# Six token groups of a gated unit join the attention phase's event loop, and the first loads of the phase before it move ahead

## The chip, the cores and the metric

The kernel runs on one core of one Trainium2 chip. The metric is the device time of one execution of the whole program, in microseconds (us). The core has five engines with a queue of instructions each, worked off in order: TensorE (PE in the profile; PEld is its weight load), VectorE (DVE), ScalarE (ACT), GpSimd (POOL) and SyncE (SP), which here only issues transfers. Transfers (DMA) run beside them, on 16 engines of their own. A timing of this kernel tells a change of about 0.2% (5 us) from none.

## The reference, cut to what matters

One layer of a decoder trunk on 2048 tokens of width 1024, in float32. One projection feeds three groups of heads; their normed outputs are joined, multiplied by `w_out`, added to `x`, and a squared-ReLU feed-forward follows.

```python
proj = rms_norm(x, norm1_g) @ w_in
o_a = swa_sink_mixer(qa, ka, va, sinks, bias[:, :4])      # banded attention, window 128
# o_b: a state-space scan, then the gated unit:
z = gelu(y);  ab = z @ glu_w + glu_b                       # 512 -> 1024
o_b = ab[..., :512] * sigmoid(ab[..., 512:])
# o_c: compressed blocks, top-16 selected blocks, window 512, gated and summed
o_c = nsa_mixer(qc, kvc, gates, cmp_pos, cmp_w1, cmp_w2, ..., bias[:, 4:])
mixed = concat(rms_norm(o_a), rms_norm(o_b), rms_norm(o_c))
x = x + mixed @ w_out
x = x + relu(rms_norm(x) @ w_up) ** 2 @ w_down
```

## The kernel before, in words

Products on PE take float32 factors split into a high and a low part, so that one product is three matmuls (`mm3`, L70 to L74). The program is a sequence of phases.

**The front** (`phase_front`, L77) computes the projection for token groups 0 to 15 and writes its columns to DRAM as `pa`, `pb`, `pc` (L169), runs the state-space scan, and leaves the activated result `z` in on-chip memory as `u_st` (L556).

**The middle phase** (in `trunk`, L2239 to L2251) merges three lists of steps by their share of the list (`merge`, L64): the banded attention of 16 blocks of 128 tokens (`swa_steps`: `prep` loads the rows `ta` at L916 and L917 and turns them, then `log_step`, `pv_step`, `close`); the gated unit (`glu_steps`, L575: eight loads of weights, L587 to L592, two of the bias, then for each of the 16 token groups `zt`, which copies the rows on POOL (L608), turns them on PE (L611) and splits them (L614, L615), and two calls of `half`, each of 13 matmuls of 128x512 into one PSUM bank (L72 to L74, L626), followed by a tanh (L629), or by the product (L634), the square sum (L635) and the store to `ob` (L636)); and a third list of the bias tables (`bias_steps`, L677: a table `T` of 1 MB and a table `b_sel` of 0.5 MB for each of four heads, L693 and L694, and the copy of `b_cmp` on POOL, L695) and of the compressed keys (`compress_steps`, L700). Here the Tile framework orders the instructions of each engine: by priority, which is the place in the program, shifted where the code says so, and by when its model of times takes them to be ready. The matmuls of `half` are shifted back by 300 places:

```python
        with tc.high_priority(offset=-FILL_GLU):
```

PSUM has eight banks: six of the banded attention, one (`pm`) of the gated unit, and one (`pg`) which the compressed keys share with the first half-product of groups 0 to 10 (`GLU_SHARES`); groups 11 to 15 use `pm` alone.

**The mixing phase** (`phase_mix`, L1084) has its order written by an event loop (`Flow`, L995) at build time. Each piece of work is a routine (a generator) that yields the events and rings of buffers that it needs and then an operation as a triple of engine, expected time and function; the loop always takes the operation that can start first, and among those the one of lowest rank (L1052 to L1060). Its whole order on every engine is fixed (`manual_schedule`). For each block i of 128 tokens there are routines for the loads and turned heads (`front`), the compressed branch (`compressed`; from block 8 on `select` picks the blocks), the window and the selected branch (`attended`), and the output product (`finished`, `filled`: 48 matmuls into `pw`, L1656). The three branches of a block each fill one bank of the ring `po`, which has two, until a copy to `oT` (L1383) frees it. The output weights `wo` take the memory of the gated unit, so they are loaded only after `open_late` (L1120), which gives that memory back and computes the row factors from the square sums of all groups:

```python
            yield E[0]["w1"]
            yield "DVE", 5000, open_late
            fire(opened, flow.engines["DVE"])
```

`E[0]["w1"]` is the end of block 0. In `open_late` two chains of small DVE operations (L40 to L50, then L1141) read the square sums `ss_a` and `ss_b`; the second waits for the last group of the gated unit. Behind `opened` the weights are loaded in 16 pieces and split on ACT and DVE (L1169, L1170).

**The feed-forward** (`phase_up`, `phase_down`) follows.

## Time and profile before

| what | value |
| --- | --- |
| time, median of 3 runs | 2517.14 us (2515.62 to 2517.17) |
| the profiled execution's own time | 2512.47 us |
| its span in the profile | 2510.4 us |
| PE busy over the span | 2408.8 us, 96% |
| DVE, ACT, POOL busy | 71%, 53%, 41% |
| mean granted clock of PE | 0.986 |
| middle phase, about | 400 to 600 us |
| mixing phase, about | 602 to 1240 us |

Times in the profile count from the start of the span. "PEclk" is the clock that was granted to PE in a stretch, as a share of the full clock. A row of the timeline gives the start, the duration, the engine, the line of the kernel, the operation and its tiles as out<-in, and in brackets how long the engine had been idle and what released it. A row of the table of stretches gives the stretch, its length, and the busy time of each engine in it with the count of its instructions, then PEclk, the share of the transfer engines in use, and GB/s.

### The profile page before, as it was taken

The page shows a single profiled execution, that of the slowest core. Times are in us where ns is not written, and L with a number is a line of the kernel's source. Part 1 is how long each engine was busy: PE and PEld are TensorE (multiplying, and loading weights), DVE is VectorE, ACT ScalarE, POOL GpSimd, SP SyncE. Part 2 cuts the span into 40 slices and gives each one's busy share as a digit, 9 for nine tenths or more (in the row PEclk, how much of TensorE's full clock was granted, in tenths as well). Part 3 has the DMA queues.
Part 4 walks back from the last instruction along what each step waited for, and adds up shares of the span by engine and source line. Part 5 has one row for each costly group of instructions (what it writes and reads, how often), then busy time and mean ns, then how long its engine had stood idle before and what let it go on. Part 6 is the DMA issues. An engine that isn't in the chain of part 4 may idle for free.

```text
span 2510.4 us, 37968 instructions
## 1 busy us (share of the span) xinstructions
PE 2408.8 (96%) x12738; PEld 2064.4 (82%) x12738; DVE 1780.0 (71%) x3496; ACT 1322.1 (53%) x2754; POOL 1037.5 (41%) x1027
## 2 busy tenths in 40 slices
PE   8999998999699999999799999999999999999999
PEld 8899997777588888888678888788887888888887
DVE  7853875864687788878465665755557988888886
ACT  6443545754577667666455555544444444434442
POOL 0000222311243344322656775565664435445447
PEclk9999998999799999999999999999999999999999
DMA  7473325421322233211556667755448443444435
GB/s 231 141 261 108 111 91 183 114 60 47 94 72 74 78 117 114 66 60 45 182 165 192 187 198 219 215 166 156 145 128 280 145 124 98 135 135 127 127 99 197
DMA packets 402259, 344.45 MB, mean 137 GB/s; under 512 B 43622, under 2 KB 359020, under 8 KB 400112
## 3 DMA queue, kind: packets, MB, share of 16 engines
q1 hardware_dynamic: 341840, 288.44, 37.9%
q10 hardware_dynamic: 60224, 53.59, 6.8%
q8 instruction: 100, 1.64, 0.3%
q14 instruction: 95, 0.78, 0.1%
HBM read 227.39 MB, written 119.76 MB: 138 GB/s over the span
## 4 chain that ended last, share of the span: by engine, by line
PE 62%; DVE 3%; DMA 3%; issue 3%; POOL 2%; ACT 2%; ACTq 0%; SPq 0%; DVEq 0%; POOLq 0%
PE pdc L2117 7%; PE pdb L2117 7%; PE pda L2117 7%; PE pub L1938 6%; PE pw L1656 6%; PE puc L1938 6%; PE pua L1938 5%; PE pdd L2117 3%; PE pud L1938 3%; PE pos L1357 2%; PE pps L1324 2%; PE pow L1357 1%; PE pqs L1299 1%; PE pqs L1300 1%; PE ppw L1324 1%
## 5 line engine op out<-in xcount | busy, mean ns | idle before, releaser
L1784 ACT CAST v<-vr 128x512 fp32r<-128x512 f32 x224 | 139.4, 624 | 303.8 <-DMA vr<-vd 126.6
L1785 DVE TENSOR_TENSOR v<-vr,v 128x512 fp32r<-128x512 f32 x224 | 235.1, 1058 | 78.6 <-ACT v L1784 78.3
L2117 PE MATMUL pdc<-dw,v 128*128 128x512 f32 x768 | 187.2, 393 | 4.4 <-ACT dw L1784 2.8
L2117 PE MATMUL pdb<-dw,v 128*128 128x512 f32 x768 | 184.5, 389 | 0.0
L2117 PE MATMUL pda<-dw,v 128*128 128x512 f32 x768 | 184.5, 389 | 0.0
L2117 PEld LDWEIGHTS pdc<-dw,v 128*128 128x128 f32 x768 | 145.4, 190 | 36.1 <-ACT dw L1784 3.3
L546 POOL TENSOR_TENSOR t<-Q,E 128x508 f32<-128x508 f32 x16 | 22.1, 1384 | 364.5 <-PE pbt L517 251.7
L2117 PEld LDWEIGHTS pdb<-dw,v 128*128 128x128 f32 x768 | 144.1, 188 | 30.0
L2117 PEld LDWEIGHTS pda<-dw,v 128*128 128x128 f32 x768 | 144.1, 188 | 29.9
L1784 ACT CAST uh<-fs 128x512 fp32r<-128x512 f32 x124 | 76.3, 621 | 156.3 <-PE pub L1938 59.7
L1785 DVE TENSOR_TENSOR ul<-fs,uh 128x512 fp32r<-128x512 f32 x124 | 130.9, 1057 | 32.5 <-ACT uh L1784 31.9
L1909 POOL TENSOR_TENSOR fs<-ur,ur 128x512 f32<-128x512 f32 x62 | 89.1, 1437 | 156.0 <-DMA ur<-in_w_up 120.7
L1785 DVE TENSOR_TENSOR ul<-ur,uh 128x512 fp32r<-128x512 f32 x93 | 99.4, 1071 | 48.2 <-ACT uh L1784 45.5
L1656 PE MATMUL pw<-wo_h,mh 128*128 128x512 f32 x256 | 105.6, 413 | 11.1 <-ACT pw L1679 10.9
L1340 ACT CAST ths<-pps 128x512 fp32r<-128x512 f32 (+1 forms) x144 | 79.1, 563 | 64.2 <-PE pps L1324 52.9
L1954 POOL TENSOR_TENSOR ev<-e,e 128x512 f32<-128x512 f32 x64 | 90.8, 1419 | 46.1 <-ACT e L1951 19.7
L1345 DVE TENSOR_TENSOR tls<-pps,ths 128x512 fp32r<-128x512 f32 (+1 forms) x144 | 92.8, 656 | 17.2 <-ACT ths L1340 16.2
L1938 PE MATMUL pub<-fh,uh 128*128 128x512 f32 x256 | 101.3, 396 | 3.3 <-DVE e L1947 3.3
L1656 PE MATMUL pw<-wo_l,mh 128*128 128x512 f32 x256 | 104.0, 406 | 0.0
L1656 PE MATMUL pw<-wo_h,ml 128*128 128x512 f32 x256 | 103.9, 406 | 0.0
L1938 PE MATMUL puc<-fh,uh 128*128 128x512 f32 x256 | 100.3, 392 | 2.1 <-DVE eu L1947 1.9
L1938 PE MATMUL pua<-fh,uh 128*128 128x512 f32 x256 | 99.7, 389 | 1.5 <-ACT pw L1679 1.5
(556 smaller groups left out, 7788.5 us busy)
## 6 DMA issues: line engine op xcount, KB each, us to landing
vr<-vd SPq DMA_DIRECT2D x224, 256.0 KB
vd<-ev SPq DMA_DIRECT2D x128, 256.0 KB
ur<-in_w_up SPq DMA_DIRECT2D x124, 256.0 KB
vd<-e ACTq DMA_DIRECT2D x64, 256.0 KB
dr<-in_w_down SPq DMA_DIRECT2D x32, 512.0 KB
x<-in_x SPq DMA_DIRECT2D x16, 512.0 KB
mx<-in_x ACTq DMA_DIRECT2D x32, 256.0 KB
x<-mx ACTq DMA_DIRECT2D x32, 256.0 KB
```

Of the source, the lines that this page charges most:

```text
L1299: nc.tensor.matmul(pq[:, o:o + w], S["qA"][:, h], ka, start=True, stop=False)
L1324: nc.tensor.transpose(pt[:, j, hh], sls[hh][:, (b0 + j) * P:(b0 + j + 1) * P], C["ident"])
L1340: yield "ACT", cast_ns(n), lambda: nc.scalar.copy(th[:, 0:nb], pt[:, 0:nb])
L1345: t = yield "DVE", sub_ns(n), lambda: nc.vector.tensor_tensor(tl[:, 0:nb], pt[:, 0:nb], th[:, 0:nb], op=ALU.subtract)
L1357: nc.tensor.matmul(po_of(), v_of(b0 + j), tt[:, j].rearrange("p h q -> p (h q)"), start=b0 + j == 0 and n == 0, stop=b0 + j == nblk - 1 an ...
L1656: t = yield "PE", mm_ns(512), lambda: nc.tensor.matmul(pw[n], a[half][:, j], b[k][:, sl], start=k == 0 and m == 0, stop=k == NK - 1 and m ...
L1784: nc.scalar.copy(dh, src)
L1785: nc.vector.tensor_tensor(dl, src, dh, op=ALU.subtract)
L1909: nc.gpsimd.tensor_tensor(t, x, y, op=op)
L1938: nc.tensor.matmul(bank[b], w[:, k], h[o][:, k], start=first and k == 0 and n == 0, stop=k == HALF - 1 and n == 2, skip_group_check=True)
L1954: nc.gpsimd.tensor_tensor(tile_("v" + o), x, y, op=op)
L2117: nc.tensor.matmul(bank[b, q], x[:, q, j], y[:, j], start=first and j == 0 and n == 0, stop=j == 1 and n == 2, skip_group_check=True)
```

## The change

1. **First loads ahead.** The first steps of the banded attention and of the gated unit become steps `ahead`, which fetch the rows of blocks 0 and 1, the sinks and the first two pieces of the gated unit's weights. They are taken, with the four banded bias tables, ahead of all else of the phase, with the SP queue in written order and the priority raised by 700 places. The first two `prep` are raised by 250. The last store of `pc` goes out on ACT's queue and not on SP's.
2. **The bias tables of the third list come after the compressed keys,** three empty steps lead that list, and every load of `T`, `b_sel` and of the compressed keys' inputs is made to wait for a recent block of the banded attention: `after` writes one element of its target from a tile of that block, on POOL.
3. **The gated unit's setup:** the constants are filled on POOL once and not on DVE, and the bias row is copied for two partitions and not for 128.
4. **The gated unit's bank.** Both banks belong to the gated unit's pool (`pm` for the second half and the turned rows, `pg` for the first half, for all groups); the compressed keys use `pg` from there.
5. **Groups 10 to 15** leave the middle phase's list. Each becomes a routine of the event loop (`glu_rows`, `glu_out`) of rank 150 plus its number, with the same operations as before; their two banks are a ring.
6. **`opening`** waits for these six groups and not for the end of block 0. Until then the ring `po` has one bank; `open_late` adds the second.
7. **`select`** no longer waits for `opened`; its tile `pm` lies in memory that is there from the start.

```diff
-GLU_SHARES = 11
+GLU_FIRST = 10
+SWA_HOIST = 250
+FETCH_HOIST = 700
...
-                rows.append(lambda: nc.sync.dma_start(pdv[kind][s], o))
+                rows.append(lambda: (nc.scalar if (s, kind) == (T16 - 1, "c") else nc.sync).dma_start(pdv[kind][s], o))
...
+    for tag, bufs in (("z", 1), ("a", 2), ("b", 2), ("zl", 2), ("zh", 2)):
+        sp.tile([P, 512], F32R if tag in ("zl", "zh") else F32, tag=tag, name="g0" + tag, bufs=bufs)
+    raws = {}
+    def fetch(n, k):
+        raw = raws[n, k] = sp.tile([P, 512], F32, tag="a", name=f"graw{k}{n}")
+        nc.sync.dma_start(raw, glu_w[0, k * P:(k + 1) * P, 512 * n:512 * n + 512])
...
     def load(n, k):
...
-        raw = sp.tile([P, 512], F32, tag="a", name=f"graw{k}{n}")
-        nc.sync.dma_start(raw, glu_w[0, k * P:(k + 1) * P, sl])
+        if (n, k) not in raws:
+            fetch(n, k)
+        raw = raws.pop((n, k))
...
     def bias(n):
...
-        if n:
-            nc.vector.memset(ones.bitcast(F32), 1.0)
...
-        nc.vector.memset(br, 0.0)
...
-        nc.scalar.copy(bh[:, sl], br)
+        for r in (0, 32):
+            nc.scalar.copy(bh[r:r + 1, sl], br[r:r + 1])
...
-    box = {}
-    def zt(t):
-        z = sp.tile([P, 512], F32, tag="z", name=f"z{t}", bufs=1)
+    box, zs = {}, {}
+    def rows_of(t):
+        z = zs[t] = sp.tile([P, 512], F32, tag="z", name=f"z{t}", bufs=1)
...
-        pt = ps.tile([P, 4, P], F32, tag="pm", name=f"gpt{t}")
+    def bank(tag, name):
+        return ps.tile([P, 512], F32, tag=tag, name=name)
+    def turn_rows(t, pt):
+        z = zs.pop(t)
...
-            nc.tensor.transpose(pt[:, j], z[:, j * P:(j + 1) * P], C["ident"])
+            nc.tensor.transpose(pt[:, j * P:(j + 1) * P], z[:, j * P:(j + 1) * P], C["ident"])
+    def high(t, pt):
...
-        nc.scalar.copy(zh, pt)
+        box[t] = [zh, zl]
+        nc.scalar.copy(zh.rearrange("p a b -> p (a b)"), pt)
+    def low(t, pt):
+        zh, zl = (z.rearrange("p a b -> p (a b)") for z in box[t][0:2])
...
-        box[t] = [zh, zl]
+    def part(t, n, pm, k):
+        zh, zl = box[t][0:2]
+        sl = slice(512 * n, 512 * n + 512)
+        mm3(nc, pm, zh[:, k], zl[:, k], wh[:, k, sl], wl[:, k, sl], k == 0, False)
+    def last(n, pm):
+        nc.tensor.matmul(pm, ones, bh[:, 512 * n:512 * n + 512], start=False, stop=True)
+    def gate(t, pm):
+        b = sp.tile([P, 512], F32, tag="b", name=f"gb{t}")
+        nc.scalar.activation(b, pm, AF.Tanh, scale=0.5)
+        box[t].append(b)
+    def gated(t, pm):
+        a = sp.tile([P, 512], F32, tag="a", name=f"ga{t}")
+        nc.vector.scalar_tensor_tensor(a, box[t][2], 1.0, pm, op0=ALU.add, op1=ALU.mult)
+        box[t].append(a)
+    def square(t):
+        nc.scalar.activation(box[t][2], box[t][3], AF.Square, accum_out=ss[:, t:t + 1])
+    def store(t):
+        nc.sync.dma_start(obv[t], box.pop(t)[3])
+    def zt(t):
+        rows_of(t)
+        pt = bank("pm", f"gpt{t}")
+        turn_rows(t, pt)
+        high(t, pt)
+        low(t, pt)
...
     def half(t, n):
-        zh, zl = box[t][0:2]
-        p, tag = (ps_x, "pg") if t < GLU_SHARES and n == 0 else (ps, "pm")
-        pm = p.tile([P, 512], F32, tag=tag, name=f"gpm{t}{n}")
-        sl = slice(512 * n, 512 * n + 512)
+        pm = bank("pm" if n else "pg", f"gpm{t}{n}")
...
-                mm3(nc, pm, zh[:, k], zl[:, k], wh[:, k, sl], wl[:, k, sl], k == 0, False)
-            nc.tensor.matmul(pm, ones, bh[:, sl], start=False, stop=True)
+                part(t, n, pm, k)
+            last(n, pm)
...
-            b = sp.tile([P, 512], F32, tag="b", name=f"gb{t}")
-            nc.scalar.activation(b, pm, AF.Tanh, scale=0.5)
-            box[t].append(b)
+            gate(t, pm)
...
-            b = box.pop(t)[2]
-            a = sp.tile([P, 512], F32, tag="a", name=f"ga{t}")
-            nc.vector.scalar_tensor_tensor(a, b, 1.0, pm, op0=ALU.add, op1=ALU.mult)
-            nc.scalar.activation(b, a, AF.Square, accum_out=ss[:, t:t + 1])
-            nc.sync.dma_start(obv[t], a)
-    res = [lambda: load(1, 0), lambda: zt(0)] + [lambda k=k: load(1, k) for k in range(1, 4)] + [lambda: bias(1)]
+            gated(t, pm)
+            square(t)
+            store(t)
+    def ahead():
+        nc.gpsimd.memset(ones.bitcast(F32), 1.0)
+        nc.gpsimd.memset(bh.bitcast(F32), 0.0)
+        fetch(1, 0)
+        fetch(1, 1)
+    res = [ahead, lambda: zt(0), lambda: load(1, 0)] + [lambda k=k: load(1, k) for k in range(1, 4)] + [lambda: bias(1)]
...
-    for t in range(T16):
-        if t + 1 < T16:
+    for t in range(GLU_FIRST):
+        if t + 1 < GLU_FIRST:
...
-    return res
+    return res, ps, (rows_of, bank, turn_rows, high, low, part, last, gate, gated, square, store)
...
 def bias_vectors(tc, tp, ps, rel_bias, oh2, ohs, r2, rs):
...
+def after(nc, C, *ts):
+    for t in ts:
+        nc.gpsimd.tensor_scalar(t, C["gate"], 1.0, 1.0, op0=ALU.mult, op1=ALU.mult)
 def bias_steps(tc, C, B, pool, tp, rel_bias, r2w, rsw):
...
+        after(nc, C, T[0:1, 0:1], B["sel"][0:1, h, 0:1])
...
     def start(st):
...
+        w1 = box["w1"] = tp.tile([P, 16, P], F32, tag="w1", name=f"cw1{st}")
+        after(nc, C, X[0:1, 1024:1025], w1[0:1, 0, 0:1])
...
-        w1 = box["w1"] = tp.tile([P, 16, P], F32, tag="w1", name=f"cw1{st}")
...
-    nc.sync.dma_start(sk, sinks[0:1].to_broadcast([P, 4]))
...
-    nc.vector.tensor_scalar(skn, sk, -1.0, None, op0=ALU.mult)
...
-    for t in q_lo:
-        nc.gpsimd.memset(t[64:P].bitcast(F32), 0.0)
-    def prep(i):
-        ta = lp.tile([P, 512], F32, tag="ta", name=f"ta{i}")
+    rows = {}
+    def fetch(i):
+        ta = rows[i] = lp.tile([P, 512], F32, tag="ta", name=f"ta{i}")
...
+    def prep(i):
+        if i not in rows:
+            fetch(i)
+        ta = rows.pop(i)
...
+        C["gate"] = vals[i][0:1, 0, 0:1].bitcast(F32)
...
     def log_step(i, h):
...
-    res = [lambda: prep(0), lambda: prep(1)] + [lambda h=h: log_step(0, h) for h in range(4)]
+    def ahead():
+        fetch(0)
+        fetch(1)
+        nc.sync.dma_start(sk, sinks[0:1].to_broadcast([P, 4]))
+        for t in q_lo:
+            nc.gpsimd.memset(t[64:P].bitcast(F32), 0.0)
+    def first():
+        with tc.high_priority(offset=SWA_HOIST):
+            nc.vector.tensor_scalar(skn, sk, -1.0, None, op0=ALU.mult)
+            prep(0)
+            prep(1)
+    res = [ahead, first] + [lambda h=h: log_step(0, h) for h in range(4)]
...
-        ps_o = pool("m_pso", 2, space=PSUM)
+        ps_o = [pool("m_pso", 1, space=PSUM)]
...
-        R = {n: Ring(k) for n, k in (("pq", 2), ("pp", 2), ("po", 2), ("pt", 1), ("pw", 1), ("sl", 4), ("th", 2), ("oT", 1), ("ot", 1),
-                                     ("qd", 1), ("tc", 1), ("xt", 4), ("mix", 1), ("mh0", 1), ("mh1", 1), ("fill", 1), ("oc", 2))}
+        R = {n: Ring(k) for n, k in (("pq", 2), ("pp", 2), ("po", 1), ("pt", 1), ("pw", 1), ("sl", 4), ("th", 2), ("oT", 1), ("ot", 1),
+                                     ("qd", 1), ("tc", 1), ("xt", 4), ("mix", 1), ("mh0", 1), ("mh1", 1), ("fill", 1), ("oc", 2),
+                                     ("gz", 1), ("gl", 2), ("gb", 2), ("ga", 2), ("gp", 2))}
...
+        gated_all = [Event() for _ in range(NT)]
+        glu_banks = ["pm", "pg"]
+        pm = kp.tile([P, P], F32, name="pm")
...
         def open_late():
...
         def opening():
-            yield E[0]["w1"]
+            for e in gated_all[GLU_FIRST:]:
+                yield e
...
+            put(R["po"], flow.engines["DVE"])
...
+        rows_of, glu_bank, glu_turns, glu_high, glu_low, glu_part, glu_last, gate, gated, square, glu_store = glu
+        def glu_rows(t):
+            yield R["gz"]
+            yield "POOL", 670, lambda: rows_of(t)
+            yield R["gl"]
+            yield R["gp"]
+            tag = glu_banks.pop(0)
+            pt = glu_bank(tag, f"gpt{t}")
+            s = yield "PE", 4 * TURN_NS, lambda: glu_turns(t, pt)
+            put(R["gz"], s)
+            yield "ACT", cast_ns(512), lambda: glu_high(t, pt)
+            s = yield "DVE", sub_ns(512), lambda: glu_low(t, pt)
+            glu_banks.append(tag)
+            put(R["gp"], s)
+            both = Event()
+            for n in (1, 0):
+                yield R["gp"]
+                tag = glu_banks.pop(0)
+                pm = glu_bank(tag, f"gpm{t}{n}")
+                for k in range(4):
+                    yield "PE", 3 * mm_ns(512), lambda: glu_part(t, n, pm, k)
+                s = yield "PE", mm_ns(512), lambda: glu_last(n, pm)
+                spawn(glu_out(t, n, pm, tag, both), R_GLU + t, s)
+            put(R["gl"], s)
+        def glu_out(t, n, pm, tag, both):
+            if n == 1:
+                yield R["gb"]
+                s = yield "ACT", 598, lambda: gate(t, pm)
+            else:
+                yield both
+                yield R["ga"]
+                s = yield "DVE", 684, lambda: gated(t, pm)
+            glu_banks.append(tag)
+            put(R["gp"], s)
+            if n == 1:
+                fire(both, s)
+                return
+            s = yield "ACT", 820, lambda: square(t)
+            put(R["gb"], s)
+            s = yield "SP", 50, lambda: glu_store(t)
+            put(R["ga"], s + DMA_NS)
+            fire(gated_all[t], s)
...
         def landing(t, nbytes):
...
             def tile_():
...
-                    box["t"] = ps_o.tile([P, 512], F32, tag="po", name=name)
+                    box["p"] = ps_o.pop(0)
+                    box["t"] = box["p"].tile([P, 512], F32, tag="po", name=name)
...
             def half(pair, fin):
...
+            tile_.back = lambda: ps_o.append(box["p"])
...
         def combined(i, po, w, first, prev, done, name, rank):
...
+            po.back()
...
         def select(i, den):
...
-            yield opened
...
-            pm = late["fp"].tile([P, P], F32, tag="pm", name=f"pm{i}", bufs=1)
...
+            for t in range(GLU_FIRST, NT):
+                spawn(glu_rows(t), R_GLU + t, 0.0)
...
+R_GLU = 150
...
             def pool(name, bufs, **kw):
...
-            ps_x = pool("x_pg", 1, space=PSUM)
...
-            glu = glu_steps(tc, C, c_u, u_st, glu_w, glu_b, ob, ss_b, ps_x)
+            glu, ps_x, rest = glu_steps(tc, C, c_u, u_st, glu_w, glu_b, ob, ss_b)
...
-            run(b_swa)
+            with tc.manual_schedule(engines={mybir.EngineType.SP}), tc.high_priority(offset=FETCH_HOIST):
+                swa.pop(0)()
+                glu.pop(0)()
+                run(b_swa)
...
-            run(merge(swa, glu, b_nsa + c_steps))
-        phase_mix(tc, C, x, gains, B, cmp, w_out, out_norm_g, norm2_g, pd, oa_d, ob, x1, hT, sums, rr, rh_c, ss_a, ss_b, r_d, oc_d, c_u.close)
+            run(merge(swa, glu, [lambda: None] * 3 + c_steps + b_nsa))
+        phase_mix(tc, C, x, gains, B, cmp, w_out, out_norm_g, norm2_g, pd, oa_d, ob, x1, hT, sums, rr, rh_c, ss_a, ss_b, r_d, oc_d, rest, c_u.close)
...
```

5 lines of the change are left out of this document (3 added, 2 removed).

## The prediction

> **What bounds the kernel now.** I read the page first, then a table of stretches, then the timelines of the two stretches that stood out. The page:
>
> ```profile
> PE 2408.8 (96%) x12738; PEld 2064.4 (82%) x12738; DVE 1780.0 (71%) x3496; ACT 1322.1 (53%) x2754; POOL 1037.5 (41%) x1027
> PE   8999998999699999999799999999999999999999
> PEclk9999998999799999999999999999999999999999
> PE 62%; DVE 3%; DMA 3%; issue 3%; POOL 2%; ACT 2%; ACTq 0%; SPq 0%; DVEq 0%; POOLq 0%
> ```
>
> PE leads the chain of waits and is busy 96% of the span. The change adds and removes no matmul, so it can only pay where PE stands idle or runs at a lowered clock: at the two dips in the 7th and the 11th slice (a slice is 63 us), the start of the middle phase and its end. The table of stretches (columns: stretch, length, busy time of PE, PEld, DVE, ACT, POOL, then the clock, the share of transfers, GB/s):
>
> ```profile
> 400.00:410.00 10.00, 6.32 (x36) 5.78 (x34) 0.36 (x2) 1.98 (x4) 2.60 (x5) 0.91 0.78 263
> 410.00:420.00 10.00, 4.25 (x15) 2.69 (x16) 8.18 (x14) 4.65 (x13) 5.89 (x7) 0.50 0.75 232
> 420.00:430.00 10.00, 8.96 (x43) 7.46 (x44) 7.78 (x27) 6.78 (x19) 1.84 (x2) 0.73 0.46 153
> 430.00:440.00 10.00, 8.60 (x53) 6.56 (x51) 8.27 (x23) 8.28 (x26) 2.99 (x4) 1.00 0.87 305
> 440.00:450.00 10.00, 8.48 (x50) 6.41 (x50) 9.18 (x25) 7.70 (x24) 5.22 (x5) 1.00 0.94 260
> 450.00:600.00 150.00, 145.65 (x838) 119.02 (x837) 95.76 (x292) 92.48 (x284) 34.85 (x41) 1.00 0.25 67
> 600.00:610.00 10.00, 7.76 (x40) 5.46 (x40) 4.50 (x14) 4.16 (x14) 2.93 (x4) 1.00 0.17 53
> 610.00:620.00 10.00, 9.74 (x59) 7.87 (x59) 6.94 (x38) 7.05 (x32) 2.35 (x3) 1.00 0.11 28
> 620.00:630.00 10.00, 8.11 (x34) 6.36 (x33) 1.46 (x3) 3.49 (x10) 0.00 (x0) 0.84 0.07 26
> 630.00:640.00 10.00, 7.78 (x32) 5.48 (x31) 0.69 (x1) 1.92 (x4) 0.00 (x0) 0.99 0.07 26
> 640.00:650.00 10.00, 2.91 (x14) 2.08 (x12) 6.16 (x31) 0.72 (x2) 0.00 (x0) 0.86 0.53 133
> 650.00:660.00 10.00, 8.01 (x37) 7.13 (x37) 7.85 (x29) 5.68 (x17) 3.48 (x4) 0.63 0.13 33
> 660.00:670.00 10.00, 7.50 (x35) 6.80 (x35) 8.92 (x23) 8.16 (x22) 2.62 (x3) 0.66 0.43 133
> 670.00:680.00 10.00, 7.08 (x31) 5.67 (x29) 8.33 (x25) 6.72 (x22) 2.39 (x3) 0.66 0.61 190
> 680.00:690.00 10.00, 6.62 (x31) 6.29 (x32) 8.92 (x26) 8.55 (x22) 6.57 (x13) 0.74 0.26 69
> 690.00:700.00 10.00, 9.79 (x64) 8.92 (x64) 8.02 (x25) 6.92 (x21) 2.31 (x3) 0.92 0.43 133
> 700.00:1200.00 500.00, 489.22 (x3276) 434.90 (x3275) 407.53 (x1199) 341.55 (x820) 186.95 (x396) 1.00 0.24 77
> ```
>
> I call **lost** the length of a stretch less PE's busy time times its clock. 400 to 450 does 5.75 + 2.13 + 6.54 + 8.60 + 8.48 = 31.5 us of work at full clock and loses 18.5. 450 to 600 loses 4.4 in 150 (2.9%). 600 to 650 does 7.76 + 9.74 + 6.81 + 7.70 + 2.50 = 34.5 and loses 15.5. 650 to 700 does 5.05 + 4.95 + 4.67 + 4.90 + 9.01 = 28.6 and loses 21.4. 700 to 1200 loses 10.8 (2.2%). What the change can win lies in the 55 us of the three dips.
>
> **The first dip (400 to 450), parts 1 to 3.** The rows that set it:
>
> ```profile
> POOL b_cmp L695 <- DMA T<-r2w: 7.3, 1, 7.3
> PE gpt L611 <- POOL z L608: 5.1, 1, 5.1
> ```
> ```profile
> 404.20 0.60 ACT L556 ACTIVATE u_st<-py 128x512 f32<-128x512 f32 x1 [3.73 <-PE py L555]
> 408.68 0.42 SPq L916 DMA_DIRECT2D ta<-pa  x1
> 412.37 1.47 POOL L783 TENSOR_TENSOR qda<-ta,rh_a 128x768 f32<-128x768 f32 x1 [0.99 <-DMA ta<-pa]
> 419.76 0.79 PE L72 MATMUL gpm<-glu_h,zh 128*128 128x512 f32 x1 [2.50 <-DVE zl L615]
> 421.91 0.45 PE L840 MATMUL pqa<-wa,qAa 128*128 128x128 f32 x1
> ```
>
> The gated unit's rows are complete at 404.8, but POOL sits 7.3 us in the copy of `b_cmp`, which waits for the 1 MB of `T`; PE waits 5.1 us behind that. With `T` behind the compressed keys this wait is gone. The rows `ta` are issued at 408.68, behind the last store of `pc`; from the start of `qda` (412.37) to the first logits (421.91) the chain takes 9.5 us. Issued ahead, `ta` is limited by memory and banks that the front still holds, which the trace doesn't show. So the gain lies between 0 (they come free only as the front ends, and `z` finds another wait) and 9.5 (the whole chain overlaps the front). The 5.1 us are nearest, and some of the chain: I take **7**. What stays of the dip is the tight DVE of 420 to 450 (7.8 to 9.2 of 10), whose eight weight splits stay. The filled constants (part 3) take work from DVE and give four short copies to ACT; with DVE as the tight one I cost it at 0, bounds 1 either way. The store on ACT's queue stands behind the last copies of the front, with nothing urgent after it: 0.
>
> `T` and `b_sel` move to the last fifth of the phase, where the transfers are a quarter busy (0.25 in the row of 450 to 600). One head's cycle:
>
> ```profile
> 435.37 0.37 SPq L693 DMA_DIRECT2D T<-r2w  x1
> 441.58 0.84 POOL L695 TENSOR_SCALAR b_cmp<-T 128x128 f32<-128x128 f32 x1
> ```
>
> That is 6.2 us from issue to copy, and with one buffer for `T` four of them in a row take 24.8. The first is gated by one of the last `prep`, some four blocks before the end; a block takes about 150/16 = 9.4 us, so some 37 us are there for it. I cost it at 0; if that cover is gone it is the slower rival below. The twelve one-element copies of `after` go to a POOL that is busy 34.85 of 150 us, and it is the waiting in POOL's queue that would count, not they.
>
> **The second dip (600 to 650), parts 4 to 6.** What stands there now:
>
> ```profile
> 626.03 0.50 PE L72 MATMUL gpm<-glu_h,zh 128*128 128x512 f32 x1 [1.40 <-DVE zl L615]
> 637.16 0.39 PE L72 MATMUL gpm<-glu_h,zh 128*128 128x512 f32 x1
> 638.54 0.39 PE L626 MATMUL gpm<-glu_bh,glu_ones 128*128 128x512 f32 x1
> 649.95 0.38 PE L1300 MATMUL pqc<-kcB,qB 96*128 96x16 f32 x1 [7.09 <-DVE qB L1228]
> ```
> ```profile
> 642.95 0.69 DVE L634 SCALAR_TENSOR_TENSOR ga<-gb,gpm 128x512 f32<-128x512 f32 x1 [7.36 <-PE gpm L626]
> 643.55 0.17 DVE L41 TENSOR_SCALAR r_a<-rah 128x16 int32<-128x16 int32 x1
> 649.15 0.74 DVE L1228 SCALAR_TENSOR_TENSOR qB<-ptqc,gains,qA 64x512 fp32r<-64x512 f32 x1
> ```
>
> The event loop put `open_late` behind block 0 without knowing of the last groups. So DVE's queue holds the chain of the row factors (643.55 to 649.15, 5.6 us), the chain stands behind the last product of the gated unit, and block 1's `qB` stands behind the chain. From 623 to 643 PE has only the gated unit, one bank deep, and then 7.09 us nothing. After the change the loop knows the six groups. Six matmuls start in 638.54 - 637.16 = 1.38, so 0.23 each; a group is 26 of them, 6.0 us, and its four turns half a microsecond: six groups are some 39 us of PE work that waits for nothing in the attention, spread over blocks 0 to 2, whose chains leave holes. With such a mixture 450 to 600 loses 2.9%, or 1.5 us in 50: the upper bound of the gain is 15.5 - 1.5 = 14. The chain of 5.6 us on DVE stays, when the groups are used up, so PE may wait for most of it: I leave 3 us. The gain is 15.5 - 1.5 - 3 = **11**. The lower bound is 4: the same end of the last group and the same chain, with only the 7 us before them filled.
>
> Moving work also empties the middle phase: ten groups beside 16 blocks instead of about 12 to its end. DVE needs 95.76 and PE 145.65 of its 150 us; six groups fewer still leave PE the busier one. I cost it at 1 us, bounds 0 and 5. One `po` bank lets a block's three branches follow one another; each handover waits for the copy to `oT`:
>
> ```profile
> 659.30 0.59 ACT L1383 COPY oTs<-pos 128x512 f32<-128x512 f32 x1 [0.45 <-ACT wo_h L1169]
> ```
>
> 0.59 and the way there and back, for three branches of three blocks, lengthen the chain by some 6 to 9 us, hidden by the 39 us of the six groups; without that cover it would be paid, at most 9. I cost it at 0.
>
> **The third dip (650 to 700).**
>
> ```profile
> L1170 DVE SCALAR_TENSOR_TENSOR wo_l<-oraw,wo_g,wo_h 128x512 fp32r<-128x512 f32 x16 | 13.9, 911 | 0.0
> ```
> ```profile
> 695.32 0.47 PE L1656 MATMUL pw<-wo_h,mh 128*128 128x512 f32 x1
> ```
>
> Between `open_late` and the first output product (46 us from 649.15) PE has only attention, DVE is busy 7.9 to 8.9 of 10, and 13.9 us of that split `wo`. None of it goes away: `opened` now waits for six groups, so it comes no sooner, by my count near 650 again, but one block further on. Two of the 21.4 us lost are idle time (11.0) and clock (10.4). The clock was lowered by the idle 7.09 us ahead. If DVE is the limit, a full clock gains nothing (0); if it isn't, 10.4. I take **4**, as DVE stands nearer to its limit than PE. `select` without `opened` concerns blocks from 8 on, long after `opened`: 0.
>
> Here a rule can be weighed. The Trainium skill (TensorE: Matmul & The Clock Gate, "What's actually happening") has the clock halve only after an idle window of about 3.4 us. The row of 620 to 630 shows 0.84 after a wait of 1.40 us, so this trace doesn't bear that out: short waits are enough. By the rule the third dip would run at full clock once the 7.09 us are gone, and the sum below would be 27.4 in place of 21.
>
> **The sum**, against the profiled execution's 2512.47 us: 7 + 11 + 4 - 1 = 21, so 2491.5. The median of the runs is 2517.14, 4.7 above the profiled one; on that scale 2496.
>
> **The rivals.**
>
> *More is won.* The early chain overlaps wholly (9.5), the groups fill the second dip (14) and the clock stays up in the third (10.4): 33.9, so 2483. For it: the lowered clock follows directly on the 7.09 us. Against: DVE at 8.9 of 10.
>
> *The hole only moves.* The six groups are used up before DVE's chain and the weights of `wo`; attention alone then loses again what was won, the 11 of the second dip and the 4, and a gain of 7 less 1 is left: 2511. For it: the third dip is of that kind, and ranks 160 to 165 put the groups ahead of block 2's attention (rank 180 and up), so nothing is kept for the time after. Against: blocks 2 and 3 have wider rows than 1.
>
> *The early loads do nothing,* that is the change doesn't do this part: 21 - 7 = 14, so 2503. For it: the front's tiles may hold the memory until 406.
>
> *Slower: the late tables.* The copies of `b_cmp` stand in POOL's queue with the last `qda` and block 0's turned heads of the mixing phase behind them. If the first `T` goes out only as the last block closes, the whole 24.8 us lie open, and PE comes back at a clock of 0.5 to 0.73 for 13 us (4.5 more lost in 410 to 430): 29.3 - 21 = 8.3 slower, 2525. It turns slower when the loads start less than about 8 us before that close (29.3 - 8.3 = 21). Against: the gate is a block of the list's last fifth, and I count 37 us.
>
> **How the numbers follow.** The forecast has 0.50 (own range 2487 to 2506), more won 0.16, the moved hole 0.16, early loads for nothing 0.09, the late tables 0.09. The range must hold most of these: from 2479 (upper bounds of all terms and a little of the hand-over to the feed-forward, whose order also shifts) to 2517. 0.2% is about 5 us, what a measurement of this kernel can tell. Faster by more than that (below 2512): the forecast, more, the early loads' case and a third of the moved hole, 0.80. Within: the rest of the moved hole, 0.11. Slower: the late tables, 0.09.
>
> **What would show it.** In the profile after: `gpt` no longer waits for `b_cmp`, and the first `pqa` comes some 7 us sooner after the last product of the front; the rows of the gated unit's last groups lie among those of blocks 0 to 2 with no 7 us hole; DVE's chain of row factors stands behind the six groups; a dip with DVE at 8 to 9 of 10 remains before the first `pw`. Wrong it would be if POOL waits for `T` when the mixing phase starts, if the middle phase loses more than 6 us between its dips, or if the dip before `pw` grows.

## The result, and the profile after

The changed kernel takes 2487.06 us (median of 4 runs, 2486.16 to 2489.40) beside 2516.38 for the kernel before: a ratio of 0.9896, with a 95% interval of 0.9878 to 0.9914. On another chip the two gave 2486.36 and 2509.90, a ratio of 0.9903 (0.9887 to 0.9919). So the gain is 29.3 us on the first chip and 23.5 on the second. Between the two profiled executions lie 25.5 us of span (2510.4 and 2484.9).

The page after (busy times, the 40 slices, the chain of waits):

```profile
PE 2397.5 (96%) x12738; PEld 2059.6 (83%) x12738; DVE 1779.7 (72%) x3493; ACT 1321.3 (53%) x2756; POOL 1036.7 (42%) x1041
PE   8999998999899999999799999999999999999999
PEclk9999999999899999999999999999999999999999
PE 68%; DVE 3%; issue 3%; POOL 2%; DMA 2%; ACT 1%; ACTq 0%; SPq 0%; DVEq 0%; POOLq 0%
```

As many matmuls as before, and of the two lowered clocks in the slices one is left, in the 11th. The table of stretches after, with the columns of the prediction's:

```profile
400.00:410.00 10.00, 7.36 (x45) 6.88 (x44) 1.64 (x7) 3.70 (x10) 6.57 (x10) 1.00 0.38 102
410.00:420.00 10.00, 8.97 (x32) 6.86 (x32) 7.14 (x20) 6.64 (x17) 3.56 (x3) 0.50 0.77 222
420.00:430.00 10.00, 8.55 (x56) 6.74 (x55) 9.30 (x31) 8.46 (x27) 2.76 (x2) 0.99 0.44 92
430.00:440.00 10.00, 7.61 (x39) 6.05 (x39) 9.75 (x25) 8.28 (x25) 3.31 (x4) 0.83 0.34 69
440.00:450.00 10.00, 8.90 (x56) 7.01 (x56) 8.23 (x25) 8.86 (x26) 3.53 (x4) 1.00 0.67 199
450.00:600.00 150.00, 142.44 (x830) 118.01 (x830) 97.41 (x312) 93.29 (x298) 40.30 (x57) 1.00 0.34 106
600.00:640.00 40.00, 38.78 (x233) 33.25 (x232) 24.67 (x88) 24.60 (x82) 10.33 (x14) 1.00 0.12 38
640.00:650.00 10.00, 8.82 (x49) 7.29 (x47) 4.87 (x19) 4.87 (x14) 1.48 (x2) 1.00 0.30 66
650.00:660.00 10.00, 5.27 (x27) 5.25 (x27) 8.13 (x34) 2.83 (x7) 0.73 (x1) 0.66 0.53 159
660.00:670.00 10.00, 7.15 (x33) 5.92 (x32) 8.75 (x29) 8.33 (x25) 3.49 (x6) 0.66 0.33 107
670.00:680.00 10.00, 8.68 (x56) 7.27 (x56) 9.96 (x24) 9.87 (x23) 3.20 (x8) 1.00 0.54 177
680.00:690.00 10.00, 8.84 (x56) 7.15 (x54) 8.82 (x20) 7.63 (x21) 7.28 (x14) 1.00 0.55 180
690.00:700.00 10.00, 8.43 (x47) 7.78 (x48) 7.66 (x26) 7.12 (x22) 2.08 (x3) 0.83 0.07 26
700.00:1200.00 500.00, 483.38 (x3212) 428.61 (x3212) 402.66 (x1157) 336.07 (x788) 192.44 (x397) 1.00 0.28 87
```

By the prediction's measure of lost time (length less PE's busy time times clock, summed over pieces of 10 us):

| stretch | lost before | lost after | won | forecast |
|---|---|---|---|---|
| 400 to 450 | 18.5 | 14.5 | 4.0 | 7 |
| 450 to 600 | 4.4 | 7.6 | -3.2 | -1 |
| 600 to 650 | 15.5 | 2.4 | 13.1 | 11 |
| 650 to 700 | 21.4 | 17.3 | 4.1 | 4 |
| 700 to 1400 | 29.8 | 25.6 | 4.2 | 0 |

The measure isn't exact: PE's busy time times clock over the whole span is 2384 us before and 2380 after, for the same matmuls. It finds some 22 of the 25.5 us; a few us either way say nothing. A sharper clock is the start of each block's front in the mixing phase (`qA` on ACT). From block 8 on, the work between two of them no longer differs from before. Before:

```profile
606.09 0.69 ACT L1226 ACTIVATE qA<-ptqc,gains 128x512 fp32r<-128x512 f32 x1 [0.50 <-PE ptqc L790]
833.92 0.69 ACT L1226 ACTIVATE qA<-ptqc,gains 128x512 fp32r<-128x512 f32 x1
```

After (the last one is block 15; before it stands at 1130.69):

```profile
587.44 0.69 ACT L1350 ACTIVATE qA<-ptqc,gains 128x512 fp32r<-128x512 f32 x1 [1.54 <-PE ptqc L845]
809.83 0.70 ACT L1350 ACTIVATE qA<-ptqc,gains 128x512 fp32r<-128x512 f32 x1
1105.84 0.69 ACT L1350 ACTIVATE qA<-ptqc,gains 128x512 fp32r<-128x512 f32 x1
```

At block 8 the changed kernel is 24.1 us ahead, at block 15 24.9, at the end 25.5: nearly everything is won before block 8. I call this start **front 8** below and compare the experiments by it. Two profiles of the changed kernel itself gave 809.8 and 810.6.

What the third dip consists of, after (rows of the timeline; the bracket of the last one is PE's wait):

```profile
645.59 0.69 DVE L651 SCALAR_TENSOR_TENSOR ga<-gb,gpm 128x512 f32<-128x512 f32 x1 [3.95 <-PE gpm L642]
647.75 0.17 DVE L42 TENSOR_SCALAR rah<-ss_a 128x16 f32<-128x16 f32 x1
653.90 0.17 DVE L1218 TENSOR_SCALAR r_c<-r_c 128x16 f32<-128x16 f32 x1
653.99 0.69 DVE L1522 TENSOR_TENSOR otc<-ptoc,wc 128x512 f32<-128x512 f32 x1
654.73 1.11 PE L845 MATMUL ptqc<-c_ident,qdc 128*128 128x128 f32 x4 [5.91 <-DVE otc L1522]
```

The 29 operations of the row factors stand on DVE from 647.75 to 654.07, 6.3 us, behind the last product of the gated unit and ahead of `otc`; PE waits 5.91 us, and the rows of 10 us up to 670 have a clock of 0.66.

### The profile page after: what moved, and what is told of

Its sections match the earlier page's. It is cut to its first block, busy times and chain, and to the rows that moved or that the text cites. A ratio compares the mean times of both kernels' runs of the same rounds, so it can differ in the third digit from the quotient of the medians.

```text
span 2484.9 us, 37987 instructions
## 1 busy us (share of the span) xinstructions
PE 2397.5 (96%) x12738; PEld 2059.6 (83%) x12738; DVE 1779.7 (72%) x3493; ACT 1321.3 (53%) x2756; POOL 1036.7 (42%) x1041
## 4 chain that ended last, share of the span: by engine, by line
PE 68%; DVE 3%; issue 3%; POOL 2%; DMA 2%; ACT 1%; ACTq 0%; SPq 0%; DVEq 0%; POOLq 0%
PE pdc L2245 7%; PE pdb L2245 7%; PE pda L2245 7%; PE pub L2066 6%; PE puc L2066 6%; PE pw L1781 6%; PE pua L2066 6%; PE pdd L2245 3%; PE pud L2066 3%; PE pos L1481 2%; PE pps L1448 2%; PE pow L1481 1%; PE pqs L1424 1%; PE pqs L1423 1%; PE ppw L1448 1%
## 5 line engine op out<-in xcount | busy, mean ns | idle before, releaser
L1913 DVE TENSOR_TENSOR v<-vr,v 128x512 fp32r<-128x512 f32 x224 | 240.4, 1082 | 78.3 <-ACT v L1912 78.1
L1781 PE MATMUL pw<-wo_h,mh 128*128 128x512 f32 x256 | 105.5, 412 | 10.4 <-ACT pw L1804 10.2
```

The source lines that it names most:

```text
L1781: t = yield "PE", mm_ns(512), lambda: nc.tensor.matmul(pw[n], a[half][:, j], b[k][:, sl], start=k == 0 and m == 0, stop=k == NK - 1 and m ...
L1913: nc.vector.tensor_tensor(dl, src, dh, op=ALU.subtract)
```

## The experiments

Each is the changed kernel with the edit named. Front 8, the span of the profile, and the ratio to the kernel before on the same chip:

| kernel | edit | front 8 | span | ratio (95%) |
|---|---|---|---|---|
| before | | 833.9 | 2510.4 | 1 |
| changed | | 809.8 | 2484.9 | 0.9896 (0.9878 to 0.9914) |
| a2 | none, another chip | 810.6 | 2484.2 | 0.9903 (0.9887 to 0.9919) |
| e1 | no early loads, tables early | 815.5 | 2492.1 | 0.9932 (0.9920 to 0.9944) |
| e3 | tables early | 816.1 | 2495.4 | 0.9942 (0.9931 to 0.9954) |
| e6 | no early loads | 808.6 | 2482.6 | 0.9902 (0.9886 to 0.9918) |
| e7 | tables early, compression in place | 818.4 | 2493.9 | 0.9943 (0.9927 to 0.9960) |
| e2 | no group as a routine | 820.2 | 2494.3 | 0.9950 (0.9938 to 0.9962) |
| g13 | three groups | 820.1 | 2496.9 | 0.9938 (0.9921 to 0.9954) |
| e9 | eight groups | 809.5 | 2485.5 | 0.9908 (0.9890 to 0.9926) |
| e4 | row factors step by step | 808.0 | 2479.9 | 0.9894 (0.9881 to 0.9907) |
| e5 | row factors on POOL | 812.9 | 2483.8 | 0.9895 (0.9879 to 0.9912) |
| e8 | row factors behind the splits | 815.3 | 2487.9 | 0.9924 (0.9908 to 0.9939) |
| e10 | row factors ahead of the splits | 807.5 | 2478.8 | 0.9887 (0.9870 to 0.9903) |

Front 8 and the span are those of one run, the ratio is that of the medians. The profiled run of e4 lay 1.4 us below the median of its kernel, those of e3 and g13 2.4 and 4.2 above, and that of the kernel before 3.9 below; so a difference of a few us between fronts should be read beside the ratio.

The unedited kernel was run beside e5, e6 and g13, to have one chip for all four.

> The changed kernel itself, without an edit, so that the kernels beside it are compared on one chip. The last comparison gave 0.9896 of the kernel before. Expected of every theory: 0.9885 to 0.9907 of the kernel before on this chip too.

It came as expected.

### Early loads and late tables: four corners and a control

e1, neither of the two:

```diff
-            with tc.manual_schedule(engines={mybir.EngineType.SP}), tc.high_priority(offset=FETCH_HOIST):
-                swa.pop(0)()
-                glu.pop(0)()
-                run(b_swa)
+            run(b_swa)
+            swa.pop(0)()
+            glu.pop(0)()
...
-        fetch(0)
-        fetch(1)
...
-        fetch(1, 0)
-        fetch(1, 1)
...
-            run(merge(swa, glu, [lambda: None] * 3 + c_steps + b_nsa))
+            run(merge(swa, glu, b_nsa + c_steps))
```

Besides, `first` has lost its raised priority, `nsa` and `start` their `after`, and the last store of `pc` is on SP's queue.

> The changed kernel with its early loads and its late tables undone: the rows of the first two blocks, the gated unit's first weights and the four tables of the sliding window are loaded where the steps need them, T and b_sel stand first in the list again, without the copies that hold them back, and the last store of pc is on SP's queue. The six routines, the two banks and the one po bank stay. The changed kernel measured 2487.1, the kernel before 2516.4. Theory (the terms add up, the early part is worth what the stretch 400 to 450 shows, 4 us, up to the 7 of my forecast): 2491 to 2494, POOL again waits about 7 us for T ahead of z. Rival one (the early loads are worth nothing, the stretch 400 to 450 only cuts the same work elsewhere): 2487 within 2. Rival two (the early part carries the gain, the groups only move the hole): 2505 or more.

Measured 2493.20 beside 2509.55 on that chip: what e1 keeps, the gated unit's setup, the banks, the routines and the free selection, is 18.4 us at front 8, and the rest of the change 5 to 6 more. In the ratio the rest is 0.29 to 0.36% (7 to 9 us), at the theory's upper end of 7 and above. The four corners say which half of the early part it is. e3 takes the early loads with the early tables:

```diff
-            run(merge(swa, glu, [lambda: None] * 3 + c_steps + b_nsa))
+            run(merge(swa, glu, b_nsa + c_steps))
...
-        after(nc, C, T[0:1, 0:1], B["sel"][0:1, h, 0:1])
...
-        after(nc, C, X[0:1, 1024:1025], w1[0:1, 0, 0:1])
```

> The changed kernel with T and b_sel first in the list of the middle phase again, and without the copies that hold them and the compression's loads back; the early loads of rows and weights stay. Theory (the wait of z behind the copy of b_cmp was what the first dip lost): POOL waits for T before z again, PE about 5 us behind it, 2490 to 2492. Rival one (the early loads alone do it, the place of the tables is free): 2487 within 1.5. Rival two (the late tables cost something in the middle phase, POOL waits 9.7 us for T there): 2482 to 2485.

And e6 keeps the late tables and undoes only the early loads (e1 without its last hunk, and with `after`):

> The changed kernel with only its early loads undone: rows, weights and the sliding window's tables are loaded where the steps need them, the last store of pc is on SP's queue, while T and b_sel stay at the end of the middle phase and the compression's loads keep their hold. It is the fourth corner beside the changed kernel (both), the routines alone (neither, 0.9932) and early loads with early tables (0.9942). Theory (the 4 MB of T and b_sel, not the time at which the first loads are issued, is what the start of the middle phase lost): 0.989 to 0.991, like the changed kernel. Rival one (both are needed, the one without the other is nothing): 0.993 to 0.9945. Rival two (they add up, half each): about 0.9915.

e3 came out like e1 (0.9942 and 0.9932; fronts 8 at 816.1 and 815.5), and e6 like the changed kernel on its chip (2485.50 and 2486.36; 808.6 and 810.6). So the early loads show no worth, with either place of the tables, and the late tables are worth 5.5 us (e3 to a2) to 6.9 (e1 to e6) at front 8. By the ratios the same two steps are 0.39% and 0.30% (10 and 7.5 us); the intervals leave room for both readings. The theory on e3 had the place of the wait wrong: in e1 PE waits 3.5 us for `z` again, in e3 no wait of `z` came back, and the cost was as large without it. With the tables first the compression had also slid back; its first product with `cw` came at 496.3 in place of 459.6. e7 keeps the place of its steps in the list (the product comes at 468.1) and moves the tables alone:

```diff
-            run(merge(swa, glu, [lambda: None] * 3 + c_steps + b_nsa))
+            idle = [lambda: None]
+            run(merge(swa, glu, idle * 3 + c_steps + idle * 4, b_nsa + idle * (len(c_steps) + 3)))
...
-        after(nc, C, T[0:1, 0:1], B["sel"][0:1, h, 0:1])
```

> The changed kernel with T and b_sel at the start of the middle phase, not held back, while the steps of the compression keep the places that they have in the changed kernel (when the tables were put first before, the compression also slid back: its first matrix product with cw came at 496 in place of 460). Early loads as in the changed kernel. Theory one (the gain of the late tables is the place of the compression, whose matmuls fill PE in 450 to 500): 0.989 to 0.991 of the kernel before, like the changed kernel. Theory two (it is the 4 MB of tables and their copies themselves, at the start of the phase): 0.9935 to 0.995.

Measured 2494.68, 0.9943: theory two, with front 8 at 818.4, 8 us behind a2. The early tables themselves, and not the place of the compression, are the cost. The waits of e7 between 400 and 500 (engine, who waited for what, total, times, longest):

```profile
POOL b_cmp L748 <- DMA T<-r2w: 9.3, 4, 3.9
PE ptqa L844 <- POOL qda L837: 5.5, 3, 3.6
DVE b_w L749 <- DMA b_sel<-r2w: 4.4, 1, 4.4
```

With the early loads `z` no longer stands behind the copy of `b_cmp`, but the next thing in POOL's queue does, `qda`; and DVE, the tight engine of this stretch, stands 4.4 us in its own copy of the table. In the changed kernel none of these three is among the waits over half a microsecond there. Part of the loss lies in 450 to 480: 5.7, 5.3 and 5.0 us in e1, e3 and e7, and 1.5 in the changed kernel (1.2 in the kernel before, which has other steps there). How the cost divides between POOL's queue, DVE's queue and the transfers themselves isn't settled by these runs.

### How many groups

e2 has all sixteen groups in the middle phase; the late tiles open behind block 0, as before:

```diff
-GLU_FIRST = 10
+GLU_FIRST = 16
...
-            for e in gated_all[GLU_FIRST:]:
+            for e in gated_all[GLU_FIRST:] or [E[0]["w1"]]:
                 yield e
```

> The changed kernel with all 16 groups of the gated unit in the middle phase and none as routines; the late tiles open behind block 0 as before. The early loads, the late tables and one po bank up to the opening stay. Theory (terms add up): 4 to 7 better than before from the first dip, the second and third dips back as before, so 2509 to 2513. Rival one (early part worth nothing): 2516 within 2. Rival two (the single po bank costs, up to 9, since no groups hide it): 2516 to 2525 although the first dip is short. Rival three (early part carries the gain): below 2500.

Measured 2496.84, 12.7 us below the kernel before on its chip, and 13.7 us at front 8. That is below the 2500 of rival three; but the kernel before is faster on this chip too (2509.55 beside 2516.38), and counted from that it lies between the theory (4 to 7) and rival three (16 or more). Of the 13.7 us 6.7 are there at front 0 (599.4 in place of 606.1), about what the late tables were worth above. 6.4 more come between front 2 (655.1 in place of 661.7) and front 3 (684.3 in place of 697.3), where I had expected nothing:

```profile
620.00:630.00 10.00, 10.00 (x46) 8.19 (x44) 0.69 (x1) 1.92 (x4) 0.00 (x0) 1.00 0.07 26
630.00:640.00 10.00, 3.02 (x14) 2.47 (x12) 7.60 (x42) 2.57 (x12) 0.00 (x0) 0.76 0.56 134
640.00:650.00 10.00, 8.42 (x33) 6.73 (x34) 8.41 (x27) 6.88 (x21) 2.17 (x3) 0.50 0.33 103
```

Before, PE was busy 8.11 and 7.78 in 620 to 640 with only the gated unit to do, at a clock of 0.84 in the first; here it is 10.00 at full clock until the groups end, and `r_a` begins at 630.99 in place of 643.55. By the code, groups 11 to 15 had one PSUM bank before and have two now, in e2 too. That fits the rows: 620 to 640 lost 5.5 us before, with PE's waits there for `zl`, `gb` and `ga`, which read that bank (the longest 1.4 us). No run changed the banks alone, so it is read, not shown. In e2 too PE's hole stands behind the row factors (630 to 640): PE waits 5.9 us there for the `qB` that follows them.

The routines themselves are then the step from e2 to the changed kernel, 10.4 us at front 8. g13 and e9 change their number (`GLU_FIRST` = 13 and 8):

> The changed kernel with three groups of the gated unit as routines and thirteen in the middle phase, in place of six and ten. Theory (what counts is whether the holes up to the opening are filled; before, 15.5 us were lost there and three groups are 18 us of work): within 4 us of the changed kernel, 600 to 650 loses 2 to 6. Rival one (every group moved brings its share): half of the 17 us that the six brought, 8 us slower than the changed kernel. Rival two (the middle phase pays for groups moved out of it, 450 to 600 loses 3 more in the changed kernel): 2 to 3 us faster than the changed kernel.

> The changed kernel with eight groups of the gated unit as routines and eight in the middle phase, in place of six and ten. None gave 0.9950 of the kernel before, three 0.9938, six 0.9903. Theory one (each group moved is work for PE where it would wait, and the attention alone is still short of it): about 3 to 5 us faster than six, 0.988 to 0.989. Theory two (with six the holes up to the opening are full, 600 to 650 loses 2; more only moves the opening and the weights of wo back): 0.990 to 0.991. Rival (the middle phase is short of work for PE with eight): 450 to 600 loses more than 10, 0.992 or more.

Three gave 2494.50 and front 8 at 820.1; eight gave 2486.54 and 809.5, no better than six. For three that is 8.1 us slower than six on the same chip, the number of rival one, and my "within 4 us" was wrong. Whether the gain is in proportion to the groups, as that rival had it, these runs don't tell: by the front three are no better than none, but the profile is of the slowest of six runs between 2490.70 and 2498.65, and the interval of the ratio holds both half the gain of six and none of it. For eight theory two holds. With three, in that run:

```profile
640.00:650.00 10.00, 3.10 (x15) 2.68 (x14) 8.72 (x41) 3.13 (x11) 0.39 (x1) 0.67 0.57 159
650.00:660.00 10.00, 7.63 (x34) 7.10 (x35) 8.22 (x28) 6.85 (x23) 3.38 (x4) 0.67 0.32 105
660.00:670.00 10.00, 7.92 (x45) 7.10 (x44) 8.15 (x22) 8.97 (x23) 3.36 (x10) 0.80 0.42 133
670.00:680.00 10.00, 5.78 (x29) 5.04 (x27) 8.37 (x18) 7.40 (x19) 4.27 (x4) 0.71 0.37 120
```

The groups' last matmul is at 636, and the stretch behind it is nearly as bad as it was before: 7.9, 4.9, 3.7 and 5.9 us lost in a row. PE's longest wait in it, 6.1 us, is again behind the row factors. In this run the rival of the moved hole holds. Why six shorten the stretch and three don't isn't settled.

### The third dip

e4 issues the row factors one operation at a time, the half from `ss_a` before the opening:

```diff
-            rsqrt_into(nc, sm, ra, ss_a, 1.0 / 256, NT, "ra")
-            rsqrt_into(nc, sm, rc, ss_b, 0.25 / 512, NT, "ra")
...
+        def factors():
+            for y, ss, scale in ((ra, ss_a, 1.0 / 256), (rc, ss_b, 0.25 / 512)):
+                if y is rc:
+                    yield opened
...
+                for op in ops:
+                    yield "DVE", 210, op
...
-            yield "DVE", 5000, open_late
...
+            t = yield "SP", 100, open_late
```

The last two lines are a second change, in e5, e8 and e10 as well: without the chain, `open_late` is for the event loop a short operation on SP, and `opened` comes that much sooner in its reckoning. What this does alone no run shows.

> The changed kernel with the chain of the row factors (29 operations on DVE, 6.3 us in one piece behind the last gated group) issued one operation at a time, the half from ss_a before the opening, so that other work can stand between them. Nothing is left out. Theory (the 5.9 us in which PE waits for otc behind this chain, and the clock of 0.66 that follows for some 20 us, are the third dip's cause): the hole and most of the lowered clock go, 8 to 12 us, 2475 to 2479. Rival one (DVE is the bound of 650 to 700 with the split of wo; the chain's operations are still there): 2484 to 2487. Rival two (only the idle time goes, the clock stays low for another reason): about 2481.

The half from `ss_a` ran at 563 to 566. The other half still came in one piece, since its rank (60) put it ahead of the attention's work. PE's waits in 640 to 700:

```profile
PE ptqc L845 <- DVE otc L1546: 3.1, 1, 3.1
PE pow L1505 <- ACT thw L1488: 1.3, 1, 1.3
```

The wait follows the piece: 6.3 us of chain and 5.9 of wait, 3.4 and 3.1. But front 8 came only 2 to 3 us sooner (808.0), and the ratio fell by less than the intervals can tell (0.9894 beside 0.9896 and 0.9903), far from the 8 to 12 us expected. e5 puts both halves on POOL (`yield "POOL", 250, op`):

> The changed kernel with the whole chain of the row factors on POOL, one operation at a time, the half from ss_a before the opening; DVE does none of it. Nothing is left out. With the half from ss_a moved ahead, the chain on DVE fell from 6.3 to 3.4 us, PE's longest wait for otc from 5.9 to 3.1, and the lost time of 600 to 720 from 19.7 to 15.4. Theory (the hole is as long as the piece that stands on DVE): the wait goes, another 3 to 5 us are won, 8 to 10 below the changed kernel beside it, about 0.986 of the kernel before. Rival one (with DVE's queue free the next late thing, the splits of wo on ACT and DVE or the factors' way over memory, holds PE as long): no further gain, 0.9885 to 0.989. Rival two (POOL's chain comes later and holds mix and with it pw): pw begins later than 667, 0.990 or more.

2484.36 beside 2486.36, and a ratio of 0.9895, between rival one (up to 0.989) and rival two (from 0.990): as rival one has it, no gain that the intervals can tell, and front 8 even came 2.3 us later than in a2. The first output product came at 675.3, later than the 667 of rival two, but in a2 it comes at 676.2. DVE was free, and `thw` came late in its place:

```profile
654.89 0.34 ACTq L1749 DMA_DIRECT2D mix<-oc_d  x1
655.28 0.37 ACT L1488 CAST thw<-ppw 128x256 fp32r<-128x256 f32 x1 [4.77 <-POOL r_c L1239]
655.70 0.58 PE L1505 MATMUL pow<-thw,vw 128*128 128x256 f32 x1 [3.84 <-ACT thw L1488]
```

ACT issues the loads of `wo` and of `mix` in its own order, and the cast stood behind them for 4.8 us: seven issues took 3.2, and 1.9 lie ahead of the last, which went out only as the chain on POOL ended (654.9). So the chain still had a part in it. e8 was to take both away: the half from `ss_b` at a lower rank, and the loads of `mix` for block 0 on SP's queue.

```diff
+            spawn(factors(0), 60, 0.0)
+            spawn(factors(1), R_FACTORS, 0.0)
...
+R_FACTORS = 400
...
-                nc.scalar.dma_start(mix[:, 0:256], oa_d[rows])
+                q = nc.scalar if i else nc.sync
+                q.dma_start(mix[:, 0:256], oa_d[rows])
```

> The changed kernel with the chain of the row factors step by step on DVE, the half from ss_a ahead of the opening, the half from ss_b behind the product otc and the block's other small work in DVE's queue, and with the three loads of mix for block 0 on SP's queue, so that ACT doesn't stand in them. When only one of these was done, PE's 5.9 us were replaced by 3.1 us behind the rest of the chain and 1.3 us behind thw (chain on DVE), or by 3.8 us behind thw, whose ACT stood 4.8 us in the issue of mix (chain on POOL), and the time fell by 2 us. Theory one (these waits take each other's place, both gone the hole closes and the clock stays up): 640 to 700 loses under 10 in place of 19, 0.986 of the kernel before or less. Theory two (with 16 splits of wo DVE and ACT are the limit of this stretch, a wait taken away comes back elsewhere): 0.9885 to 0.990.

The rank went too far: the event loop put the chain behind the splits of `wo` as well, not only behind `otc`. The factors were stored at 698.3 in place of 654.8, and the first output product came at 711.9 in place of 676.2: 0.9924. So this run says what late factors cost, and nothing on its two theories. e10 has the rank at 205:

> The kernel before this one in the study, with the chain at a lower rank number (205 in place of 400): there it had fallen behind the 16 splits of wo too, r_c was stored at 698 in place of 655, the first output product came at 712 in place of 676, and the time was 0.9924. Now the half from ss_b stands behind otc and the small work of blocks 1 and 2, and ahead of the next qB and the splits. The loads of mix for block 0 stay on SP's queue. Theory one (the wait for otc and ACT's stand in the loads of mix take each other's place; with both gone the third dip shortens): first pw at or before 669, 640 to 700 loses under 13, 0.986 to 0.988 of the kernel before. Theory two (attention alone leaves PE waiting here: chains of one block through DVE and ACT beside the splits): 640 to 700 loses 15 to 19 again, 0.989 to 0.991.

Measured 2479.51, 0.9887; front 8 at 807.5, the first output product at 669.7. PE's waits in 640 to 700:

```profile
PE pow L1508 <- ACT thw L1491: 3.0, 2, 2.8
PE pqc L1450 <- DVE nms L1427: 2.3, 1, 2.3
PE ptkc L845 <- POOL qdc L838: 2.3, 1, 2.3
```

The wait for `otc` is gone, and three others stand in its place; 640 to 700 loses 16.9 us, beside 18.1 in a2. By the loss that is theory two (15 to 19); the ratio lies between the two ranges. In this stretch PE waits in turn for whichever of DVE, ACT and POOL is late, and one chain taken away is worth 2 to 3 us at front 8. The 2.8 us for `thw` stand once more behind ACT's own issues: three loads of `wo`, 3.1 us from 647.75. No run moved these to another queue, so that remedy is open. e10 has the lowest ratio and the shortest span of the study, 5.4 us below a2, but its interval overlaps the changed kernel's.

## Why the prediction was right, and where not

The forecast was 2496 on the scale of the runs and 2491.5 on that of the profile; measured were 2487.1 and 2487.0. Half of the 9 us is the scale: the median before lay 4.7 us above its profiled execution, the median after on it. The other half is in the terms. The measured time lies at the lower edge of the forecast's own range (2487 to 2506).

- **The first dip, 7.** About right in size by the fronts, wrong in cause, so the size is in part luck. The late tables are worth 5.5 to 6.9 us at front 8 (7.5 to 10 by the ratios), the early loads nothing that shows (e6). I had read the wait of `z` as the thing removed and added some of the chain from `qda` to the first logits; that chain did come 9.1 us sooner (first `pqa` at 412.76 in place of 421.91), and e6, without the early loads, has it at 414.6 and ends as early. In e7 the waits stand at whatever comes next in the queues of POOL and DVE; that these waits are the whole cost is not shown. In the stretch itself only 4.0 show, against the kernel before.
- **The middle phase, -1.** Mis-sized: 450 to 600 loses 7.6 in place of 4.4, more than the 6 that I named as a sign of error. My reason, fewer groups to fill it, isn't it: e2 has all sixteen there and loses 7.8, and e9 with eight loses 6.0. What else does it stays open; the 3.2 us are near what the measure can tell.
- **The second dip, 11.** 13.1 measured, near my upper bound of 14, since DVE's chain, for which I had left 3 us, now stands for the most part behind 650. Two things that I had as one are in it: by e2 some 6 us come without any routine, for which the second bank of the last groups is the likely cause, and 10.4 us at front 8 with them.
- **The single `po` bank, 0.** Nothing speaks against it, but the case that I priced, three blocks on one bank without cover, no run has: in e2, without routines, one bank serves block 0 alone, and its front 1 follows front 0 by 14.3 us, beside 13.8 before.
- **The third dip, 4.** 4.1 measured; that it fits so closely is luck, as the measure isn't that good. Idle time went from 11.0 to 11.6 us and what the lowered clock cost from 10.4 to 5.7, so the gain is all in the clock, about half of what I had as its most. A full clock throughout wasn't put to the test, since 5.91 us of wait took the place of the 7.09. The reason, DVE near its limit, holds in part: it is a sequence of waits for DVE, ACT and POOL in turn (e4, e5, e10), and taking one away brought 2 to 3 us at front 8 (e4, e10) or none (e5). "One block further on, near 650 again" was right: the chain starts at 647.75 (643.55 before).
- **Selection, 0.** No run had it alone; nothing in the traces speaks against it.
- **The late tables' place, 0.** Right: the first `T` went out at 507.4, the last `b_cmp` was copied at 542.0, 34.6 us in place of my 24.8, and the mixing phase's first `ptqc` came at 586.8. POOL stood 9.7 us in these copies between 440 and 600, and no wait of PE followed on them.
- **700 to 1400** won 4.2 by a measure that is good to a few us; between the fronts 8 and 15 it is 0.8. I had it at 0.

**The rivals.** *More is won* named the amount best (2483), for reasons of which one came in full, the filled second dip; the chain of the first dip came sooner by nearly the 9.5 us, which was worth nothing by e6. *The hole only moves* is what three groups do, and in part six: the 5.9 us behind the row factors are the 7.09 of before, one block further on. *The early loads do nothing* was true of the loads; I had given the tables' gain to it as well. *The late tables* as the slower case had 44 us to spare.

## What to carry to other kernels

Price a bulky transfer at the start of a busy phase by every in-order queue that holds a copy of it: here the early tables, not the loads that were issued late, cost 5.5 us or more, the waits stood in POOL's and DVE's copies and behind them, and issuing the urgent loads earlier didn't help. Work kept as filler pays up to the point where the holes are full (six groups here; eight brought no more). Where PE waits in turn for three engines, the longest wait of a profile is no measure of what its removal is worth: 5.9 us of wait and a lowered clock were 2 to 3 us at front 8.
